# A batched fp32 matmul on one core: converting loads from GpSimd in place of plain loads and VectorE casts

## The chip, the cores and the metric

The kernel runs on one core of a Trainium2 chip. The metric is the device time of one execution in microseconds (us), as the median of several runs. The engines are called TensorE (PE, with its weight loads as PEld), VectorE (DVE), ScalarE (ACT), GpSimd (POOL) and SyncE (SP). Transfers between the chip's memory (HBM) and the on-chip memory (SBUF) run on 16 DMA engines; matmul results arrive in PSUM.

## The reference

```python
def setup_inputs():
    batch, m, k, n = 16, 512, 768, 1024
    return {
        "x": np.random.randn(batch, k, m).astype(np.float32),
        "y": np.random.randn(batch, k, n).astype(np.float32),
    }

def reference(x, y):
    return np.einsum('bkm,bkn->bmn', x, y).astype(np.float32)
```

For each of 16 batches, out = x^T y, with a contraction of 768. In fp32, one batch has 1.57 MB of x, 3.15 MB of y and 2.10 MB of output.

## The kernel before

The contraction index is split as k = p * 6 + ko: partition p holds six neighbouring rows of x (one run of 12 KB) and of y (24 KB). The output row is m = p * 4 + mo, so that partition p holds four whole output rows (16 KB). The lines that make these views (x_v, y_v, o_v) stand above the loops.

The loop over batches b first asks for both loads on SyncE's queue (L56 x into `xs`, L57 y into `ys`, fp32, two buffers each). From batch 4 on (LAG = 4) it then asks on the same queue for the store of batch b - 4 (L50), so that the queue holds loads and stores in one written order; four finished batches wait in `o_sb`, which has five buffers. After the loop the stores that are left are asked for. The order on each engine is the order of the program (a manual schedule).

VectorE turns fp32 into bf16: x in one cast (L62), y in two halves (L65), into `x_sb` and `y_sb`, two buffers each. A batch has eight groups (mo of 4, nt of 2), each with six matmuls of 128x128 by 128x512 (L74, contraction innermost) into one of eight PSUM tiles. ScalarE copies each group into `o_sb` (L76).

Of the kernel before, what the change touches and what calls it, by code (L numbers as in the profile page):

```python
# [1 line left out]

_os.environ.setdefault("NEURON_RT_ULTRASERVER_MODE", "4")

# [1 line left out]

# [4 lines left out]


@with_exitstack
def kernel(
    ctx: ExitStack,
    tc: tile.TileContext,
    x: bass.AP,
    y: bass.AP,
    out: bass.AP,
):  # L20
    nc = tc.nc
    P = 128
    FP32 = mybir.dt.float32
    BF16 = mybir.dt.bfloat16

    B, K, M = x.shape
    _, _, N = y.shape
    KT = K // P
    MT = M // P
    NF = 512  # L30
    NT = N // NF

    x_v = x.rearrange("b (p ko) m -> b p ko m", ko=KT)
    y_v = y.rearrange("b (p ko) n -> b p ko n", ko=KT)
    o_v = out.rearrange("b (p mo) n -> b p mo n", mo=MT)

    xs_pool = ctx.enter_context(tc.tile_pool(name="xs_pool", bufs=2))
    ys_pool = ctx.enter_context(tc.tile_pool(name="ys_pool", bufs=2))  # L40
    x_pool = ctx.enter_context(tc.tile_pool(name="x_pool", bufs=2))
    y_pool = ctx.enter_context(tc.tile_pool(name="y_pool", bufs=2))
    o_pool = ctx.enter_context(tc.tile_pool(name="o_pool", bufs=5))
    psum = ctx.enter_context(tc.tile_pool(name="psum", bufs=8, space=bass.MemoryType.PSUM))
    LAG = 4

    o_tiles = {}

    def store(b):
        nc.sync.dma_start(o_v[b], o_tiles.pop(b)[:])  # L50

    with tc.manual_schedule():
        for b in range(B):
            xs = xs_pool.tile([P, KT, M], FP32, name="xs")
            ys = ys_pool.tile([P, KT, N], FP32, name="ys")
            nc.sync.dma_start(xs[:], x_v[b])  # L56
            nc.sync.dma_start(ys[:], y_v[b])  # L57
            if b >= LAG:
                store(b - LAG)
            x_sb = x_pool.tile([P, KT, M], BF16, name="x_sb")  # L60
            y_sb = y_pool.tile([P, KT, N], BF16, name="y_sb")
            nc.vector.tensor_copy(x_sb[:], xs[:])  # L62
            for h in range(2):
                ks = slice(h * KT // 2, (h + 1) * KT // 2)
                nc.vector.tensor_copy(y_sb[:, ks], ys[:, ks])  # L65
            x_w = x_sb[:].rearrange("p k (j mo) -> p k mo j", mo=MT)
            o_sb = o_pool.tile([P, MT, N], FP32, name="o_sb")
            o_tiles[b] = o_sb
            for mo in range(MT):
                for nt in range(NT):  # L70
                    ns = slice(nt * NF, (nt + 1) * NF)
                    ps = psum.tile([P, NF], FP32, name="ps")
                    for kt in range(KT):
                        nc.tensor.matmul(ps[:], x_w[:, kt, mo], y_sb[:, kt, ns],  # L74
                                         start=(kt == 0), stop=(kt == KT - 1))
                    nc.scalar.copy(o_sb[:, mo, ns], ps[:])  # L76
            if False:
                store(b)
        for b in sorted(o_tiles):
            store(b)  # L80


# [1 line left out]
_INS = ['x', 'y']  # L84
_OUTS = [((16, 512, 1024), 'float32')]


# [23 lines left out]
```

## Time and profile before

| what | value |
|---|---|
| median of 3 runs | 261.84 us (261.81 to 262.11) |
| the profiled execution's own time | 261.84 us |
| its span, first to last instruction | 260.1 us |
| PE busy | 192.3 us, 768 matmuls, mean 413 ns |
| DVE busy | 83.0 us, 48 casts |
| ACT busy | 76.4 us, 128 copies of 587 ns |
| DMA | 109.18 MB, mean 420 GB/s |

The page of a profile gives busy times by engine, the span in 40 equal slices (each digit is a busy share in tenths), the DMA queues with packets, megabytes and share of the span, and the chain of work that ended last, followed backwards. Matmuls are pipelined, so that the mean of one holds waiting too. A table of stretches gives for each window its length, the busy time and count of PE, PEld, DVE, ACT and POOL, and then the granted TensorE clock, the DMA share and GB/s. SPq is SyncE's work of asking for transfers.

### The profile page before, as it was taken

How to read it: one execution, taken by the hardware profiler on the slowest of the kernel's cores; microseconds unless marked ns; L12 is line 12 of the kernel's file. 1: busy time of each engine (PE TensorE's matmuls, PEld its weight loads, DVE VectorE, ACT ScalarE, POOL GpSimd, SP SyncE). 2: the span in 40 equal slices, each digit the busy share in tenths (PEclk: the TensorE clock that was granted, in tenths of full speed). 3: DMA queues.
4: the chain of work that ended last, by engine and by line, in shares of the span. 5: the costliest groups of instructions: out<-in, count | busy, mean ns of one | idle time of the engine just before them, and what ended most of it. 6: DMA issues, size and time to landing. Idle time of an engine off the chain costs nothing.

```text
span 260.1 us, 1877 instructions
## 1 busy us (share of the span) xinstructions
PE 192.3 (74%) x768; PEld 89.3 (34%) x768; DVE 83.0 (32%) x48; ACT 76.4 (29%) x129; POOL 0.2 (0%) x4
## 2 busy tenths in 40 slices
PE   0059999896947939599597886939779395895950
PEld 0014555353523514235143342514334142351420
DVE  0271643525213252222524215252132522225000
ACT  1003444342421403314123241413324042141330
POOL 0000000000000000000000000000000000000000
PEclk9999999999997998959779797997999899796895
DMA  7999999999999999999999999999999999999995
GB/s 299 427 423 420 438 433 427 431 369 422 430 430 432 432 430 435 430 432 423 433 435 421 438 422 438 429 427 437 435 424 424 432 431 430 437 425 432 431 408 242
DMA packets 6921, 109.18 MB, mean 420 GB/s; under 512 B 768, under 2 KB 768, under 8 KB 768
## 3 DMA queue, kind: packets, MB, share of 16 engines
q1 hardware_dynamic: 6912, 109.05, 98.5%
q8 instruction: 6, 0.10, 0.1%
q14 instruction: 3, 0.02, 0.0%
HBM read 75.50 MB, written 33.55 MB: 419 GB/s over the span
## 4 chain that ended last, share of the span: by engine, by line
DMA 80%; DVE 10%; PE 5%; DVEq 1%; SPq 0%; issue 0%; ACT 0%
DMA ys<-in_y_dram 80%; DVE y_sb L65 10%; PE ps L74 5%; DVEq L106 1%; SPq L56 0%; ACT o_sb L76 0%; SPq L57 0%; DVEq L65 0%
## 5 line engine op out<-in xcount | busy, mean ns | idle before, releaser
L74 PE MATMUL ps<-y_sb,x_sb 128*128 128x512 bf16 x768 | 192.3, 413 | 58.4 <-DVE y_sb L65 58.4
L74 PEld LDWEIGHTS <-x_sb 128*128 128x128 bf16 x768 | 89.3, 118 | 160.9 <-issue 47.5
L76 ACT COPY o_sb<-ps 128x512 f32<-128x512 f32 x128 | 75.2, 587 | 174.1 <-PE ps L74 174.1
L65 DVE CAST y_sb<-ys 128x3072 bf16<-128x3072 f32 x32 | 54.9, 1757 | 89.4 <-DMA ys<-in_y_dram 89.4
L62 DVE CAST x_sb<-xs 128x3072 bf16<-128x3072 f32 x16 | 28.2, 1760 | 66.2 <-DMA xs<-in_x_dram 55.2
L76 ACT ACT_TABLE_LOAD x1 | 1.3, 1283 | 0.7 <-PEq L95 0.7
L95 POOL MEMSET const-uint8-127<- 128x1 uint8 x1 | 0.1, 103 | 0.0
L95 POOL MEMSET const-bfloat16-1.0<- 128x1 bf16 x1 | 0.1, 102 | 0.0
L95 POOL MEMSET const-float32-1.0<- 128x1 f32 x1 | 0.1, 100 | 0.0
L95 POOL MEMSET const-float32-0.0<- 128x1 f32 x1 | 0.1, 99 | 0.2 <-issue 0.2
## 6 DMA issues: line engine op xcount, KB each, us to landing
ys<-in_y_dram SPq DMA_DIRECT2D x16, 3072.0 KB, 28.1
out_dram<-o_sb SPq DMA_DIRECT2D x16, 2048.0 KB, 32.6
xs<-in_x_dram SPq DMA_DIRECT2D x16, 1536.0 KB, 29.7
```

Source lines behind the costliest of these rows:

```text
L62: nc.vector.tensor_copy(x_sb[:], xs[:])
L65: nc.vector.tensor_copy(y_sb[:, ks], ys[:, ks])
L74: nc.tensor.matmul(ps[:], x_w[:, kt, mo], y_sb[:, kt, ns], start=(kt == 0), stop=(kt == KT - 1))
L76: nc.scalar.copy(o_sb[:, mo, ns], ps[:])
L95: nc = _bacc.Bacc("TRN2", target_bir_lowering=False, num_devices=1)
L106: with _tile.TileContext(nc) as tc:
```

## The change

The loads go to GpSimd's queue and write bf16 straight into `x_sb` and `y_sb`: the transfer converts. The fp32 tiles `xs` and `ys` and the VectorE casts are gone. `x_sb` and `y_sb` have four buffers in place of two, `o_sb` four in place of five. Each batch's store is asked for on SyncE's queue as soon as the batch is finished, with no lag. VectorE takes the PSUM copies of the left half (nt = 0), ScalarE keeps those of the right half. The views of x, y and out and the matmul loop are as they were.

```diff
-    xs_pool = ctx.enter_context(tc.tile_pool(name="xs_pool", bufs=2))
-    ys_pool = ctx.enter_context(tc.tile_pool(name="ys_pool", bufs=2))
-    x_pool = ctx.enter_context(tc.tile_pool(name="x_pool", bufs=2))
-    y_pool = ctx.enter_context(tc.tile_pool(name="y_pool", bufs=2))
-    o_pool = ctx.enter_context(tc.tile_pool(name="o_pool", bufs=5))
+    x_pool = ctx.enter_context(tc.tile_pool(name="x_pool", bufs=4))
+    y_pool = ctx.enter_context(tc.tile_pool(name="y_pool", bufs=4))
+    o_pool = ctx.enter_context(tc.tile_pool(name="o_pool", bufs=4))
     psum = ctx.enter_context(tc.tile_pool(name="psum", bufs=8, space=bass.MemoryType.PSUM))
-    LAG = 4
-
-    o_tiles = {}
-
-    def store(b):
-        nc.sync.dma_start(o_v[b], o_tiles.pop(b)[:])
 
     with tc.manual_schedule():
         for b in range(B):
-            xs = xs_pool.tile([P, KT, M], FP32, name="xs")
-            ys = ys_pool.tile([P, KT, N], FP32, name="ys")
-            nc.sync.dma_start(xs[:], x_v[b])
-            nc.sync.dma_start(ys[:], y_v[b])
-            if b >= LAG:
-                store(b - LAG)
             x_sb = x_pool.tile([P, KT, M], BF16, name="x_sb")
             y_sb = y_pool.tile([P, KT, N], BF16, name="y_sb")
-            nc.vector.tensor_copy(x_sb[:], xs[:])
-            for h in range(2):
-                ks = slice(h * KT // 2, (h + 1) * KT // 2)
-                nc.vector.tensor_copy(y_sb[:, ks], ys[:, ks])
+            nc.gpsimd.dma_start(x_sb[:], x_v[b])
+            nc.gpsimd.dma_start(y_sb[:], y_v[b])
             x_w = x_sb[:].rearrange("p k (j mo) -> p k mo j", mo=MT)
             o_sb = o_pool.tile([P, MT, N], FP32, name="o_sb")
-            o_tiles[b] = o_sb
...
-                    nc.scalar.copy(o_sb[:, mo, ns], ps[:])
-            if False:
-                store(b)
-        for b in sorted(o_tiles):
-            store(b)
+                    eng = nc.vector.tensor_copy if nt == 0 else nc.scalar.copy
+                    eng(o_sb[:, mo, ns], ps[:])
+            nc.sync.dma_start(o_v[b], o_sb[:])
```

## The prediction

> **What bounds the kernel now.** I read the page first: the busy shares, the slices, the DMA queues and the chain.
>
> ```profile
> span 260.1 us, 1877 instructions
> PE 192.3 (74%) x768; PEld 89.3 (34%) x768; DVE 83.0 (32%) x48; ACT 76.4 (29%) x129; POOL 0.2 (0%) x4
> ...
> DMA  7999999999999999999999999999999999999995
> ...
> q1 hardware_dynamic: 6912, 109.05, 98.5%
> ...
> DMA 80%; DVE 10%; PE 5%; DVEq 1%; SPq 0%; issue 0%; ACT 0%
> ```
>
> The DMA engines are full from the second slice to the last but one, and one hardware queue carries all 109.05 MB. TensorE is next at 74%, with 58.4 us of its idle time ended by the VectorE cast of y, which itself waits for the y load (89.4 us in the table of waits). So compute follows the loads.
>
> Then the table of stretches, cut where the traffic changes: loads only, loads with stores, stores only, the end.
>
> ```profile
> 2.50:7.00 4.50, 0.00 (x0) 0.00 (x0) 0.10 (x1) 0.00 (x0) 0.00 (x0) 1.00 0.98 415
> 7.00:40.00 33.00, 23.75 (x99) 11.68 (x100) 15.47 (x9) 9.13 (x16) 0.00 (x0) 1.00 1.01 431
> ...
> 52.00:235.00 183.00, 144.06 (x573) 66.41 (x572) 58.84 (x34) 56.35 (x96) 0.00 (x0) 0.90 1.01 428
> 235.00:240.00 5.00, 2.87 (x7) 1.00 (x8) 3.43 (x2) 0.00 (x0) 0.00 (x0) 0.63 0.99 424
> 240.00:251.00 11.00, 10.67 (x43) 4.77 (x40) 0.00 (x0) 4.40 (x8) 0.00 (x0) 0.86 1.00 427
> ...
> 253.00:260.00 7.00, 0.00 (x0) 0.00 (x0) 0.00 (x0) 0.00 (x0) 0.00 (x0) 0.52 0.61 257
> ```
>
> The last three columns are granted clock, DMA share and GB/s. The rate is the same for loads alone (431), for the mix (428) and for stores alone (427). A byte costs the same in either direction, and no stretch shows a faster one. Most telling are 235 to 251: the last load has landed, the last batch is being computed, and the DMA engines are still full, with stores held back for this.
>
> Last, SyncE's queue in order of time and the end of the chain:
>
> ```profile
> 80.41 0.33 SPq L57 DMA_DIRECT2D ys<-in_y_dram  x1
> ...
> 96.22 0.33 SPq L57 DMA_DIRECT2D ys<-in_y_dram  x1
> ...
> 207.32 44.33 SPq L50 DMA_DIRECT2D out_dram<-o_sb  x5
> ```
> ```profile
> 206.94 28.08 DMA ys<-in_y_dram
> ...
> 235.12 1.76 DVE y_sb L65
> 236.88 1.68 DVEq L106
> 238.56 0.04 issue
> 238.60 12.09 PE ps L74 x45
> 250.69 0.02 issue
> 250.71 0.59 ACT o_sb L76
> ```
>
> One batch takes 15.81 us (96.22 - 80.41): 4.72 MB in and 2.10 MB out, 6.82 MB at 431 GB/s. The last five stores are issued after the last load, from 207.32 on; four of them (8.4 MB, 19.6 us at 428 GB/s) are the cover under which batch 15 is cast and multiplied.
>
> **The change part by part.** Neither the views of x, y and out nor the tiles' layouts differ: the lines that make partition-major runs are unchanged context. What changes is who converts, who issues, and when the stores go.
>
> *Casts removed.* 48 VectorE casts, 83.0 us busy. All but the last lie under transfers. On the path only the tail counts: from the last y byte (235.03) to the first matmul (236.94) 1.9 us, and the second half's cast delays the next matmuls to 238.60. Without it, matmuls start when y lands.
>
> *Evictions split.* 64 of 128 evictions go from ScalarE to VectorE. No row shows VectorE reading PSUM. ScalarE's 128x512 copy takes 587 ns; VectorE's cast of 3072 elements takes 1757 ns, in proportion 293 ns for 512. Between 0.3 and some 1.2 us (twice the ScalarE row) all values are hidden by the 1.3 us between two groups. The last group is nt == 1 and stays on ScalarE, 0.59 us. Cost nothing; I take 0.6 us for one.
>
> *Loads move from SyncE's queue to GpSimd's, and convert on the way.* GpSimd does nothing today (0.2 us), so nothing queues behind its waits but later loads. Its wait becomes the one for a free x_sb or y_sb, four batches deep: TensorE needs about 11.6 us per batch against 15.8 us of traffic, so the buffer is long free. 32 issues: a SyncE issue takes 0.33 to 0.42 us; on GpSimd I allow from that to ten times as much, 4 us, still under the 7.9 us per load that the pace demands. Only the first is exposed: +1 us taken, 0 to 4 in the range. The Trainium skill, page "DMA: Bandwidth & Descriptors", section "Specifications", puts the first byte at about 1 us from GpSimd against 0.6 from SyncE: by that the start would cost 0.4 us, and no run here shows it.
>
> *The rate of a converting load* is the unknown that decides. The HBM side still reads 75.50 MB; only the SBUF side halves, to 37.75 MB. Bounds: if the time goes by the bytes read, nothing changes (176 us of loads at 428 GB/s). If it goes by the bytes written, loads take 88 us. If conversion costs, the nearest figure is reading and then writing in turn, 113.3 MB, 265 us; half the rate is 353 us. I take the bytes read: every stretch shows an engine's stream at its limit whatever it carries, and a stream that converts must still take in every fp32 byte. The same page, section "Where 436 GB/s comes from", calls the 16 SBUF ports the bottleneck. By that rule, read literally, 37.75 + 33.55 = 71.3 MB would pass them in 164 us and TensorE would bound the kernel. The trace has only transfers of equal size on both sides and cannot tell the two apart. The rule that speaks against the change stands under "Latency and other measured facts": two of the sixteen engines are usually slower when GpSimd issues, with a cause that it calls a guess and no size. By that the sum would grow, by an amount that no run here shows.
>
> *Stores no longer held back.* Store b is issued as soon as batch b is evicted, in a queue of its own. In the steady state that moves nothing: the engines are full either way, at 15.8 us per batch. At the end it takes the cover away. Step by step:
> - By 235.03 before had moved 0.17 + 1.87 + 14.22 + 5.17 + 78.32 = 99.8 MB (the stretches, rate by length).
> - Batch 14's y lands one pace, 15.8 us, ahead of batch 15's. Computing it takes 11.6 us (45 matmuls took 10.84 us in the batch from 206.97; 48 take 11.6; 10.4 at full clock, 12.9 by the last batch's rate) plus 0.6. Store 14 so starts 3.6 us ahead of the last load's landing and moves some 0.8 MB at half the rate.
> - The last load therefore lands when 75.50 + 14 x 2.10 + 0.8 = 105.7 MB have moved: 5.9 MB more than before, at 428 GB/s 13.8 us later, 248.8. With the start, 249.8.
> - Then 11.6 us of matmuls and 0.6 of eviction: 262.0. The rest of store 14 is over 3 us into this; the DMA engines then stand idle for about 9 us. That idle stretch is the loss.
> - Store 15: issued at 251.3 in before and landed 7.9 us later, with rests of earlier stores ahead of it. Alone, 2.10 MB at 428 GB/s is 4.9 us, plus 2.4 us of latency (the first x load landed 6.1 us after its issue, of which 3.7 is its bytes). I take 7.4: 269.4. From landing to the end of the span 0.9 us, as in before: 270.3.
>
> The profiled execution itself took 261.84 us, 1.7 over its span, and equals the median of the three runs. So 270.3 + 1.7 = 272.0 us, 10.2 us or 3.9% slower. With the small terms at their ends (start 0 to 4, matmuls 10.4 to 12.9, rate of the mix 424 to 436) the case spans 266 to 280.
>
> **The rivals.**
>
> *Faster: a converting load is paid by the bytes written.* Then TensorE sets the end: x0 and y0 (2.36 MB) land at about 9 us, 768 matmuls take the 192.3 us that they take now, and eviction, last store and the rest add 10.6: 212 us. For it: nothing bounds loads but the DMA engines. Against: no stretch has loads above 431 GB/s. It decides from a small gain: the uncovered tail costs 10.2 us, 5.8% of 176 us of loads. If loads take in fp32 by more than 6% faster than today, the change wins. Chance 9%; 3% for a gain of a few per cent, ending at 254 to 261.
>
> *Slower: conversion or the second queue costs rate.* Each 10% on the loads is 17.6 us. A loss of 4 to 20% gives 279 to 306, chance 20%: two queues now share the engines, and packets may be cut smaller than today's (mean 17.7 KB, 109.05 MB over 6144 data packets). Half the rate gives 272 + 176 = 448 us, reading and writing in turn 361; together 10%. From about 7.9 us of descriptor work per load GpSimd itself would be the bound.
>
> *The change does less than its words.* Were its layout the matter, nothing would move, since the layout is already there. The time within 0.2% would need the tail's idle DMA offset by a like gain: 2%.
>
> **How the numbers follow.** A measurement of this kernel tells some 0.2% from no change. My case 56% (266 to 280), loss of rate 20%, half the rate or in turn 10%, bytes written 9%, small gain 3%, no change 2%. Faster 0.12, same 0.02, slower 0.86. The range takes in all but the two far cases (19%): 254 to 306. Predicted: 272.
>
> **What would show it.** Right: the GB/s row stays near 430 with two queues, the pace of y loads stays near 15.8 us, no stretch has DMA share below 0.95 until the last y lands near 250, and then a hole of about 9 us opens under batch 15's matmuls, followed by a store of about 7 us alone. The cast rows are gone and VectorE has 64 copies near 0.6 us. Wrong: TensorE over 85% busy (bytes written), a pace clearly over 16 us (conversion costs), GpSimd's issues as the end of the idle time, or a start more than 4 us later. If bytes are counted as written, the GB/s row will drop to some 280 at a full DMA share; the share and the pace, not that row, then decide.

## The result, and the profile after

The changed kernel takes 271.58 us (median of four runs, 270.73 to 272.61), the kernel before 261.98 us beside it. The ratio is 1.0365, 95% interval 1.0318 to 1.0413: slower by 9.6 us, where 10.2 were forecast. The profiled execution took 272.32 us, with a span of 270.1.

From the page of the changed kernel: span, DMA share in 40 slices, GB/s in 40 slices, and the two queues.

```profile
span 270.1 us, 1854 instructions
...
DMA  6999999999999999999999999999999999998607
GB/s 112 227 215 209 225 311 310 310 268 311 206 323 270 304 283 210 304 285 331 256 251 313 227 315 275 296 291 284 302 205 289 301 295 293 277 307 201 274 0 311
...
q0 software_dynamic: 4608, 37.75, 67.0%
q1 hardware_dynamic: 2304, 33.56, 29.6%
```

Read the two rows together. The GB/s fell from some 430 to between 200 and 331 once the start is over, and the DMA engines are as full as before: the row counts bytes as they are written, and a converting load writes half of what it reads. What is new are the digits 8, 6, 0 ahead of the last one: a hole before the last store. The table of stretches places it (columns behind the window: length, busy time of PE, PEld, DVE, ACT, POOL, then clock, DMA share, GB/s):

```profile
7.00:14.00 7.00, 0.00 (x0) 0.12 (x1) 0.00 (x0) 0.00 (x0) 0.00 (x0) 1.00 1.00 212
14.00:26.00 12.00, 11.12 (x44) 5.20 (x44) 2.11 (x4) 1.76 (x3) 0.00 (x0) 1.00 1.02 215
...
248.00:250.00 2.00, 0.16 (x1) 0.00 (x0) 0.00 (x0) 0.58 (x1) 0.00 (x0) 1.00 0.46 162
250.00:255.00 5.00, 4.88 (x15) 2.00 (x16) 0.69 (x1) 0.36 (x1) 0.00 (x0) 0.66 0.88 367
255.00:260.00 5.00, 5.00 (x24) 2.61 (x23) 1.38 (x2) 1.04 (x3) 0.00 (x0) 1.00 0.01 3
260.00:263.00 3.00, 2.33 (x11) 1.02 (x9) 0.69 (x1) 0.95 (x2) 0.00 (x0) 1.00 0.00 0
263.00:270.00 7.00, 0.00 (x0) 0.00 (x0) 0.00 (x0) 0.00 (x0) 0.00 (x0) 0.60 0.71 300
```

With loads alone (7 to 26) 212 to 215 GB/s are written, so 424 to 430 are read, the rate of the plain loads. From 255 to 263 nothing moves, while TensorE works. The end of the chain of waits tells the same as a sequence (start and length in us, then what ran; L57 is the matmul, L60 the copy):

```profile
201.25 48.72 DMA y_sb<-in_y_dram
249.98 0.14 issue
250.12 12.23 PE ps L57 x48
262.34 0.02 issue
262.36 0.58 ACT o_sb L60
```

In the kernel before, the y load of batch 15 landed at 235.03, with five stores still to go. Here it lands at 249.98 with two, and the second of them cannot be asked for until 263.0.

### The profile page after: what moved, and what is told of

It reads as the page before. It is cut to its first block, busy times and chain, and to the rows that moved or that the text cites. A ratio compares the mean times of both kernels' runs of the same rounds, so it can differ in the third digit from the quotient of the medians.

```text
span 270.1 us, 1854 instructions
## 1 busy us (share of the span) xinstructions
PE 191.4 (71%) x768; PEld 89.5 (33%) x768; DVE 44.3 (16%) x64; ACT 38.8 (14%) x65; POOL 17.4 (6%) x36
## 3 DMA queue, kind: packets, MB, share of 16 engines
q0 software_dynamic: 4608, 37.75, 67.0%
HBM read 75.50 MB, written 33.55 MB: 404 GB/s over the span
## 4 chain that ended last, share of the span: by engine, by line
DMA 58%; PE 31%; another core or an unknown queue 6%; issue 1%; POOL 1%; ACT 0%; POOLq 0%
DMA y_sb<-in_y_dram 58%; PE ps L57 31%; POOL x_sb L48 1%; ACT o_sb L60 0%; POOLq L76 0%
## 5 line engine op out<-in xcount | busy, mean ns | idle before, releaser
L57 PE MATMUL ps<-y_sb,x_sb 128*128 128x512 bf16 x768 | 191.4, 415 | 70.9 <-DMA y_sb<-in_y_dram 70.9
L57 PEld LDWEIGHTS <-x_sb 128*128 128x128 bf16 x768 | 89.5, 118 | 172.3 <-issue 100.5
L60 DVE COPY o_sb<-ps 128x512 f32<-128x512 f32 x64 | 44.3, 692 | 217.5 <-PE ps L57 217.5
L60 ACT COPY o_sb<-ps 128x512 f32<-128x512 f32 x64 | 37.5, 586 | 223.4 <-PE ps L57 223.4
L48 POOL DMA_DIRECT2D x_sb<-in_x_dram x16 | 8.8, 549 | 184.2 <-PE ps L57 183.4
L49 POOL DMA_DIRECT2D y_sb<-in_y_dram x16 | 8.9, 554 | 0.0
## 6 DMA issues: line engine op xcount, KB each, us to landing
out_dram<-o_sb SPq DMA_DIRECT2D x16, 2048.0 KB, 14.6
```

The costliest lines, as they stand in the source:

```text
L48: nc.gpsimd.dma_start(x_sb[:], x_v[b])
L49: nc.gpsimd.dma_start(y_sb[:], y_v[b])
L57: nc.tensor.matmul(ps[:], x_w[:, kt, mo], y_sb[:, kt, ns], start=(kt == 0), stop=(kt == KT - 1))
L60: eng(o_sb[:, mo, ns], ps[:])
```

## The experiments

Each ratio is to the kernel before, run on the same chip.

**1. The store timing alone put back.** A small transfer (`gate`) that reads y of batch b stands on SyncE's queue ahead of store b - 4, so that the store waits for that load. Stores that are held need a fifth output buffer, as in the kernel before.

```diff
+            if b >= LAG:                      # LAG = 4, o_pool bufs=5
+                gate = g_pool.tile([P, 16], BF16, name="gate")
+                nc.sync.dma_start(gate[:], y_sb[:, KT - 1, N - 16:])
+                store(b - LAG)
...
-            nc.sync.dma_start(o_v[b], o_sb[:])
```

> The change with only the store timing put back: store b - 4 is asked for on SyncE once y of batch b has landed (a 4 KB transfer that reads the last columns of that y stands ahead of it). Loads still convert and still have GpSimd's queue to themselves. Theory (the loss is the DMA hole under batch 15, because no store is left to fill it): the last y lands some 15 us earlier than in the change, near 235, the DMA share stays above 0.95 from there to 251, and the time is 262 us, within 1.5 us of the kernel before (ratio 0.995 to 1.006). Rival (the converting load or the second queue costs rate): the time stays at 268 to 273.

Measured: 263.6 us, ratio 1.0065 (1.005 to 1.008). The end of its chain, where the last y load lands at 230.83, and its table of stretches from 234 on:

```profile
184.68 46.15 DMA y_sb<-in_y_dram
...
230.96 12.22 PE ps L68 x48
```

```profile
234.00:240.00 6.00, 6.00 (x28) 3.00 (x27) 2.06 (x3) 1.18 (x2) 0.00 (x0) 0.94 1.00 424
240.00:248.00 8.00, 3.17 (x15) 1.46 (x13) 0.71 (x2) 1.17 (x2) 0.00 (x0) 1.00 1.01 434
248.00:251.00 3.00, 0.00 (x0) 0.00 (x0) 0.00 (x0) 0.00 (x0) 0.00 (x0) 0.57 1.01 431
251.00:254.00 3.00, 0.00 (x0) 0.00 (x0) 0.00 (x0) 0.00 (x0) 0.00 (x0) 0.50 0.99 426
```

Batch 15 is computed under full DMA engines, and 8 of the 9.6 us are back, with conversion, second queue and split copies all still there. The 1.7 us that stay are a little more than the 1.5 that the expectation allowed; run 5 looks for them.

**2. The reverse: the kernel before with early stores.** `store(b)` right after the batch's last copy, on ScalarE's queue; no lag.

```diff
-        nc.sync.dma_start(o_v[b], o_tiles.pop(b)[:])
+        nc.scalar.dma_start(o_v[b], o_tiles.pop(b)[:])
...
-            if b >= LAG:
-                store(b - LAG)
...
-            if False:
+            if True:
                 store(b)
```

> The kernel before with only its store timing changed: each store is asked for from ScalarE's queue right after the batch's last copy, loads stay plain fp32 on SyncE with VectorE casts. Theory (store timing alone makes the loss): last y lands near 247, then 15.7 us of cast and matmuls, 0.6 of copy, 7.4 of store, 0.9 to the end: span 271.6, time 273, ratio 1.04. Rival (the conversion in the load makes the loss): 262, ratio 1.00. Rival (half each): 267.

Measured: 273.46 us, ratio 1.0444 (1.0426 to 1.0461), span 270.8. The last y landed at 248.92, and the same hole stands in the stretches:

```profile
220.90 28.02 DMA ys<-in_y_dram
...
252.50 10.60 PE ps L72 x45
```

```profile
255.00:262.00 7.00, 7.00 (x34) 3.68 (x33) 0.00 (x0) 3.12 (x6) 0.00 (x0) 1.00 0.01 2
262.00:264.00 2.00, 1.08 (x5) 0.34 (x3) 0.00 (x0) 0.99 (x2) 0.00 (x0) 1.00 0.00 0
```

Plain loads lose too, 11.6 us against the change's 9.6, here with 3.6 us of casts between the last landing and most of the matmuls (248.92 to 252.50). The two runs together settle it: the timing of the stores makes the loss, in either kernel.

**3. Conversion undone.** GpSimd asks for fp32 loads, VectorE casts, and ScalarE copies all groups, so that the split of the copies is undone with it; stores stay early.

```diff
-            nc.gpsimd.dma_start(x_sb[:], x_v[b])
-            nc.gpsimd.dma_start(y_sb[:], y_v[b])
+            nc.gpsimd.dma_start(xs[:], x_v[b])      # xs, ys: fp32, two buffers
+            nc.gpsimd.dma_start(ys[:], y_v[b])
+            ...                                     # casts as in the kernel before
...
-                    eng = nc.vector.tensor_copy if nt == 0 else nc.scalar.copy
+                    eng = nc.scalar.copy
```

> The change with the conversion alone undone: GpSimd asks for plain fp32 loads into two-buffer tiles, VectorE casts as before, ScalarE copies all groups; stores stay early on SyncE. Theory (loads are paid by the bytes read, so converting costs and saves nothing; what it saves is the cast after the last load, 1.9 to 3.5 us): 274 us, ratio to before 1.045, 2 to 3 us above the change. Rival (conversion costs rate): below the change, 262 to 270. Rival (VectorE's casts hold up GpSimd's descriptor work): over 277, with GpSimd issues well above their 0.55 us.

Measured: 274.56 us, ratio 1.0481 (1.0446 to 1.0517), some 2.5 to 3 us above the change, as expected: the last y landed at 249.64, and the casts held the bulk of the matmuls until 253.21, 3.6 us later.

```profile
221.80 27.84 DMA ys<-in_y_dram
...
253.21 12.73 PE ps L65 x45
```

Conversion in the load is thus no loss, and it takes the casts off the tail. How much that gains is less sure: against run 10, where the change's ScalarE copies all groups as it does here (273.73 us), only 0.8 us are left. GpSimd's queue in order of time shows something else:

```profile
18.93 1.84 POOL L53 DMA_DIRECT2D ys<-in_y_dram  x1 [8.43 <-DMA xs<-in_x_dram]
20.95 0.53 POOL L52 DMA_DIRECT2D xs<-in_x_dram  x1 [0.18 <-issue]
```

A y issue that is released together with an x cast takes 1.84 us in place of 0.53, about one cast (1.76) long; all seven issues that met an x cast took 1.82 to 1.94 us. The Trainium skill, page "SBUF — State Buffer", section "Who interferes with whom", says that VectorE's two-port modes lock GpSimd out of a shared port pair, descriptor writing included; the stretched issues agree, though no run here shows in which mode the casts run. They cost no time here: a second load stood queued, and the DMA share stayed at 1.00 and 1.01 from 14 to 246 us.

**4. One written order on GpSimd's queue.** Loads, and each store four batches late, all from GpSimd; conversion kept.

```diff
+        nc.gpsimd.dma_start(o_v[b], o_tiles.pop(b)[:])   # store(b), called as store(b - 4)
```

> The change with loads and stores in one written order on GpSimd's queue, each store four batches late as in the kernel before; conversion kept. Theory (order of the bytes decides, not which engine asks): last y lands near 236, the hole is filled, 262 us, ratio 0.995 to 1.006, equal to the run with two queues and held stores within 1 us. Rival (two queues sharing the engines cost rate): 2 us or more below that run. Rival (GpSimd's queue is slower than SyncE's): 265 or more.

Measured: 264.5 us, ratio 1.0101 (1.0086 to 1.0116), where 262 was expected. The hole is filled here too; the time is 0.9 us above the run with two queues, within the 1 us that was allowed but clear of the noise, and below the 265 that a slow queue would give. From 254 on it has less traffic left than that run (share 0.42 of nine us, 3.8 us of full engines, against 0.56 of eight, 4.5), but the span ends 1.7 us later. In the table of SyncE's waits the step behind the last store takes 2.5 us against 0.7, which is about that difference. What that step is stays open.

**5. Held stores with plain loads from GpSimd**, for the 1.7 us that stay in the first run: run 1 with the edit of run 3, the copies on ScalarE included.

```diff
-            nc.gpsimd.dma_start(y_sb[:], y_v[b])
+            nc.gpsimd.dma_start(ys[:], y_v[b])               # x alike; casts as before
...
-                nc.sync.dma_start(gate[:], y_sb[:, KT - 1, N - 16:])
+                nc.sync.dma_start(gate[:], ys[:, KT - 1, N - 8:])
```

> The run with held stores and two queues (263.6 us), with its conversion undone: GpSimd asks for plain fp32 loads, VectorE casts, ScalarE copies all groups. Question: where the 1.7 us come from by which that run stays over the kernel before. Theory (converting adds some 2% to the time of a load's packets: 67.0% of 270.1 us in the change, 181.0, against 64.9% of 273.8 us, 177.7, with plain loads from GpSimd): loads take 178 us of the DMA engines' time again, and the time falls by 1.5 to 3.5 us to 260 to 262. Rival (GpSimd's later start and two queues cost them): it stays at 263 to 264.

Measured: 262.93 us, ratio 1.0036 (1.0024 to 1.0048). The fall is 0.7 us, less than the theory's 1.5. The load queue's packet time did fall, from 69.3% of 261.3 us to 68.0% of 261.1 (181.1 to 177.5 us), as the queue rows say, that of run 1 first:

```profile
q0 software_dynamic: 4608, 37.75, 69.3%
...
q0 software_dynamic: 4608, 75.50, 68.0%
q1 hardware_dynamic: 4032, 33.61, 30.4%
```

So 3.5 us of packet time became 0.7 us of time: packets overlap on an engine (the DMA share of long stretches reads 1.02 to 1.03 with converting loads, 1.01 with plain ones), and a sum of packet times is no price. Even of the 0.7 us only 0.2 lie in the span (261.3 and 261.1 us). The rest lies outside the span, where the executions of run 1 spend some 2.3 us, those of this run and of the kernel before some 1.8; why is open. With loads alone, 3 to 14 us, this run reads 418 GB/s and run 1 writes 210, so reads 420: no difference. Most of the other 0.9 us over the kernel before is the start: GpSimd's first issue comes at 1.25 us, SyncE's at 0.73, and over the first 14 us this run moves 335 GB/s against 358, 0.32 MB less, which is some 0.8 us at 428 GB/s.

**6 and 7. Less cover.** Run 1 with LAG = 2, and then also with the waiting transfer cut to one partition.

```diff
-    LAG = 4
+    LAG = 2
```
```diff
-                gate = g_pool.tile([P, 16], BF16, name="gate")
-                nc.sync.dma_start(gate[:], y_sb[:, KT - 1, N - 16:])
+                gate = g_pool.tile([1, 16], BF16, name="gate")
+                nc.sync.dma_start(gate[:], y_sb[0:1, KT - 1, N - 16:])
```

> The run with held stores and two queues, with a lag of 2 batches in place of 4. Theory (the loss is the time that the last batch's matmuls run without stores to fill it): when the last y lands, two stores are left (9.8 us), one of which can go ahead of the last batch's end only partly; last y lands near 245, a hole of about 3 us, 267 us, between 263.6 (lag 4) and 271 (no lag). Rival (any hold removes the loss, for instance by keeping queues from alternating): 263.6.

Measured: 264.04 us, ratio 1.0074 (1.0061 to 1.0088). A miss: 267 was expected. The DMA issues of that run say why (the last number is us to landing):

```profile
out_dram<-o_sb SPq DMA_DIRECT2D x16, 2048.0 KB, 26.0
...
gate<-y_sb SPq DMA_DIRECT2D x14, 4.0 KB, 16.7
```

A 4 KB transfer took 16.7 us, and the store behind it 26.0 against 14.6 in the change. When the last y landed (241.1), 7.4 MB were left (356 GB/s over the last 20.9 us): 3.5 stores, where the expectation had two and a lag of 2 holds three at most. The waiting transfer itself had held them back; run 7 tests this.

> The run with held stores and a lag of 2, with the transfer that waits for y cut from 128 partitions (128 pieces, 16.7 us to land) to one partition. Question: why that run lost only 2 us. Theory (queues alternate piece by piece; the 128 small pieces held the store behind them back, so that 7.4 MB, 3.5 stores, were left at the last landing in place of 3 at most): the thin transfer lands in a few us, a store in some 15 us as in the change, the last y lands near 244, a hole of about 3 us opens, 265 to 267 us. Rival (a lag of 2 is cover enough): 264 again.

Measured with the thin transfer: 265.57 us, ratio 1.0153 (1.0122 to 1.0183), last y at 243.9.

```profile
out_dram<-o_sb SPq DMA_DIRECT2D x16, 2048.0 KB, 16.4
...
gate<-y_sb SPq DMA_DIRECT2D x14, 0.0 KB, 5.9
```
```profile
240.00:245.00 5.00, 2.33 (x12) 1.06 (x11) 0.69 (x1) 0.59 (x1) 0.00 (x0) 1.00 0.70 261
245.00:248.00 3.00, 3.00 (x16) 1.57 (x15) 0.69 (x1) 0.59 (x1) 0.00 (x0) 1.00 0.83 339
...
254.00:257.00 3.00, 0.58 (x3) 0.10 (x1) 0.02 (x1) 0.59 (x1) 0.00 (x0) 1.00 0.83 355
```

The time is as expected, the place only partly. Of the 2.5 us without traffic, 2 lie where the loads end and the next store is not yet in (5 x 0.30 + 3 x 0.17), and 0.5 ahead of the last store.

**8. The thin transfer with a lag of 4**, run 1 with the second edit above.

> The run with held stores and a lag of 4, with the thin transfer. Theory (four stores cover the last batch however they are held): no hole, 262.5 to 263.7 us, and last y near 235. Rival (the small pieces cost DMA time, which made the 1.7 us over the kernel before): 262.2 or less, ratio 1.000 to 1.002.

Measured: 265.4 us, ratio 1.0123 (1.0108 to 1.0138), above both theories. Cover is there, but the table has this:

```profile
225.00:234.00 9.00, 6.53 (x30) 3.22 (x29) 2.08 (x3) 1.76 (x3) 0.00 (x0) 1.00 0.94 314
234.00:240.00 6.00, 5.81 (x27) 3.09 (x28) 1.38 (x2) 1.02 (x2) 0.00 (x0) 1.00 0.76 311
```

9 x 0.06 + 6 x 0.24 = 2.0 us without traffic: store 10 had drained, the last load's engines finish unevenly, and the next store is asked for only at 234.68, behind the landing of the last load:

```profile
234.68 11.02 SPq L49 DMA_DIRECT2D out_dram<-o_sb  x5
```

With the thick transfer the stores were still queued there. So a store must not only be held; it must stand in the queue before the loads run out. The kernel before does this by its one written order.

**9. The last batch shortened in the change.** Five of every six matmuls of batch 15 are left out.

```diff
-                    for kt in range(KT):
+                    last = KT if b < B - 1 else 1
+                    for kt in range(last):
```

> The change, with five of every six matmuls of the last batch left out (its contraction stops after 128 of 768), everything else alike. Theory (the loss is the last batch's matmuls, during which the DMA engines stand idle): batch 15 takes some 3 to 4 us in place of 12.2, its store starts close behind store 14, the hole is gone, 262 to 264 us. Rival (early stores, the second queue or converting loads cost time elsewhere): above 268.

Measured: 263.76 us, ratio 1.0065 (1.005 to 1.008), against 272.05 for the change beside it: 8.3 us, the length of the hole. Batch 15's matmuls took 3.59 us in place of 12.2, and the stretch that was empty is full:

```profile
250.30 3.59 PE ps L58 x8
...
255.00:260.00 5.00, 0.00 (x0) 0.00 (x0) 0.00 (x0) 0.00 (x0) 0.00 (x0) 0.50 0.99 419
```

**10 and 11. The split of the copies undone, and the change once more.**

```diff
-                    eng = nc.vector.tensor_copy if nt == 0 else nc.scalar.copy
+                    eng = nc.scalar.copy
```

> The change with the split of the copies undone: ScalarE copies all 128 groups. Theory (a copy of either engine is done within the 1.3 us between groups, and the last one is ScalarE's in both): within 0.5% of the change, 270.5 to 272.5. Rival (VectorE's copies out of PSUM disturb something): 2 us or more away from it.

Measured: 273.73 us (272.26 to 274.13), ratio 1.0436 (1.0412 to 1.0461), 2 us above the change's first four runs.

> The change itself once more, beside the other runs, for the spread of its time. Theory (its end is one chain of load, 48 matmuls, copy and store, so TensorE's granted clock in batches 14 and 15, 10.5 to 13.3 us each, goes into the time): 270.5 to 274, a spread of 1.5 us or more against 0.5 for the kernel before; the run in which ScalarE copies all groups (273.7) then lies inside it. Rival (ScalarE copying all costs 2 us): 270.5 to 272.0.

Measured: 272.05 us (270.63 to 273.61), ratio 1.0383 (1.035 to 1.0417); the kernel before beside it ranged over 0.8 us. The change's ten times spread over 3 us, and two of the four times of the copy run lie inside. A cost of ScalarE copying all, of up to some 2 us, is neither shown nor excluded. That the spread comes from TensorE's clock is argued from the chain (48 matmuls in 10.53 to 13.25 us, with nothing to hide them at the end), not shown. Run 9, with most of the last batch's matmuls gone, spreads over 1.4 us, which fits; but the mean granted clock does not tell the fastest execution here (270.63 us, 0.893) from the slowest (273.61 us, 0.895).

**12. A faster kernel?** The kernel before, with the last store cut into four.

```diff
+                if b == B - 1:
+                    if mo == 0:
+                        for e in sorted(o_tiles)[:-1]:
+                            store(e)
+                    nc.sync.dma_start(o_v[b][:, mo], o_sb[:, mo])
```

> The kernel before, with the last batch's store cut into four, each asked for as soon as its two groups are copied. Theory (before, the DMA share falls to 0.61 in the last 7 us because the last store starts only at 251.3): the DMA engines stay full until near 257, 1 to 2.5 us faster, ratio 0.990 to 0.996. Rival (its DMA engines are full to the end, so nothing is to be had, or the smaller 4 KB pieces cost it): ratio 0.998 or more.

Measured: 262.32 us, ratio 1.0014 (1.0005 to 1.0023). The theory fell, and with it the reading that the DMA engines of the kernel before are half empty at the end: the last stretch has the same share though its stores no longer start late.

```profile
253.00:260.00 7.00, 0.00 (x0) 0.00 (x0) 0.00 (x0) 0.00 (x0) 0.00 (x0) 0.53 0.61 248
```

0.61 of seven us are four us of nearly full traffic and then the end of the program: in the kernel before the share is 0.94 from 253 to 257 and 0.15 behind it. That kernel is bound by its bytes nearly to the end, and no run here beat it.

## Why the prediction was right, step by step

- *Who bounds what.* Right: full engines at an unchanged rate of bytes read until the last y lands, then the hole.
- *Rate of a converting load.* Taken as unchanged; 424 to 430 GB/s read against 431. Between runs 1 and 5 converting cost 0.7 us, 0.2 of it in the span. The rival of bytes written is excluded: 37.75 MB took as long as 75.50. So is the literal reading of the port rule (the Trainium skill, page "DMA: Bandwidth & Descriptors", section "Where 436 GB/s comes from"). The rival of lost rate is excluded above 1.7 us, what run 1 leaves for conversion, second queue and start together. (20% of 176 us is 35 us, so that rival's upper end was 307, not 306.) The rule on two slow engines under GpSimd's issue (same page, section "Latency and other measured facts") finds at most that much room; no run here shows the engines one by one.
- *Start.* 1 us taken; the first y landed at 14.84 in place of some 14.2, 0.7 us.
- *Issues and copies.* GpSimd's issues took 0.53 to 0.67 us (0.4 to 4 allowed), VectorE's copy 692 ns (600 taken).
- *Last y at 249.8.* Measured 249.98, in part by errors that cancel. Batch 14's matmuls took 13.25 us (11.6 taken), so store 14 was asked for near 248.9, not 3.6 us ahead of the landing: 0.8 MB, 1.9 us, did not go ahead. With this and the shorter start the y would have landed near 247.6. But the engines stood half idle from 248 to 250 (share 0.46, 1.1 us), since the last load's tail had nothing beside it; the other 1.3 us are not placed.
- *Tail.* 12.23 us of matmuls (11.6 taken), store 15 landed in 6.3 us (7.4 taken), hole 255 to 263 (9 us taken). Run 9 prices it at 8.3 us. Outside the span 1.7 us were taken from the kernel before, and the profiled execution has 2.2. So single terms were off by up to 1.9 us, in both directions, and that the sum came within 0.4 us of the median is in part luck, all the more as the change's own times spread over 3 us.
- *Casts off the tail.* 1.9 us was set as the floor and 3.5 shown ahead of most matmuls; run 3 shows 3.6 on its chain. Its time is 2.5 to 3 us above the change, but 0.8 above run 10, which shares its copies, so the gain in time is not sized.

## What to carry to other kernels

In a kernel bound by its transfers, as this one is, finished output that is kept back is not delay but cover: keep as many stores queued behind the last load as the last tile's computing lasts, and queue them before the loads run out. A load that converts on its way was paid here by the bytes it reads, so it removes the cast from the tail but no traffic. GB/s counted as written misleads there; read DMA share and the pace of the batches.

## What the runs showed of the hardware

- Beside another queue's loads, the number of a transfer's pieces counted for more than its bytes: 4 KB in 128 pieces took 16.7 us, a single piece 5.9, a 2 MB store in the change 14.6, and the store behind the 128 small pieces 26.0 against 16.4 us. Queues that take turns piece by piece would do this; no run here shows the turns themselves.
- A GpSimd issue released together with a VectorE cast was stretched from 0.53 to between 1.82 and 1.94 us in run 3, with the DMA engines still full (share 1.00 and 1.01).
- Converting added 3.5 us of packet time, 0.2 us of span and 0.7 us of time (run 1 against run 5).
